# A decoder layer on one core: where the MLP's first weights, its raw rows and its normed rows lie, and from which unit on the normed rows are used

## The chip, the cores and the metric

The kernel runs on one core of a Trainium2 chip. TensorE (PE in the profile) multiplies matrices and writes its sums to PSUM banks; PEld is its weight load. VectorE (DVE), ScalarE (ACT) and GpSimd (POOL) work on tiles in SBUF and PSUM, and SyncE (SP) issues the DMAs. Each engine has an instruction list of its own, fixed when the program is built, and semaphores tie the lists together. The metric is the device time of one execution in microseconds; the median of three runs is compared.

## The reference

One layer of a decoder (256 positions of 1024 channels, all float32): a norm, one input projection, three kinds of attention, a gated merge, an output projection and a residual; then the part that matters here:

```python
x = x + merged.astype(x.dtype) @ w_out[i]
x = x + conv_ffn(rmsnorm(x, norm_ffn[i]), w_up[i], conv_w[i], conv_b[i], w_down[i])
return rmsnorm(x, norm_final)

def conv_ffn(x, w_up, conv_w, conv_b, w_down):
    h = x @ w_up                       # 1024 -> 2 * 2816
    h = causal depthwise conv of width 3 over h, + conv_b
    a, u = jnp.split(h, 2, axis=-1)
    return (jax.nn.silu(a) * u) @ w_down
```

## The kernel before

**Split numbers.** Every weight arrives by DMA as a raw float32 block of 1 MB (a "unit", 128 x 2048). ScalarE writes its rounded part `whi` (`Unit.hi`, L222, two halves of 128x1024), VectorE the rest, `wlo = raw - whi` (`Unit.lo`, L226, two halves). Activations are split in the same way. A product is then three matmuls: low by high, high by low, high by high (`mm3`, L237 to L240).

**The rings.** Raw blocks and split parts come from rings of buffers: `next_tile` (L156) walks through two pools, and once attention is closed five pairs of split parts are to be had. A unit's split waits until the pair that it takes over has been read for the last time. `turns[1]` counts the pairs given out.

**Big activation buffers.** Two buffers of 128 x 4096 float32 are reused by name. `hn` (pool `acts`) holds the mixer's normed rows, high and low, which every projection of the mixer reads, the gates' at the end too (L384 to L396, L443). `parts` (pool `mix`) holds attention's split output (L491), which the branch projections read (L801). In the MLP `hn` holds the raw turned rows (the residual stream, transposed and multiplied by the norm's weight, not yet by 1/rms; L830) and `parts` holds the normed rows (L868).

**The MLP.** It has 11 units of 256 hidden channels. Unit i uses three weight units: `fa{i}` and `fu{i}` (the two halves of `w_up`) and `fd{i}` (`w_down`). For each of its two channel blocks `up` (L980) runs once on `fa` and once on `fu`, `conv` (L963) does the width-3 convolution (one activation on ScalarE, L965, two operations on VectorE, L967), silu and product follow (L1001, L1003), the result is split into `fh` and `fl` (L1006, L1007), and `later` (L760) queues its 12 products with `fd`, written to the four `acc` banks.

**Two forms of `up`.** For i < NORMED the raw turned rows are the moving operand, 24 matmuls of 256 columns, and VectorE multiplies the result by 1/rms (`by_rstd`, L861, L864). From i = NORMED on the normed rows are used: high and low part lie side by side, so that `whi` takes both in one matmul of 512 columns (L988) and `wlo` the high part in one of 256 (L990), 16 matmuls in all; ScalarE copies one half of the bank out (L996) and VectorE adds the other (L997). The normed rows are made by `norm_parts` (L874), called at i = NORMED - 1: for each of two halves one multiplication (L876), one rounding on ScalarE (L877) and one subtraction (L878).

**What sets the order.** From the last products of the output projection to the first conv of the MLP the order is written by hand (`manual_schedule`, L891 to L951; unit 0's four `up`s are `first_products` there). Before and after it a scheduler at build time sorts the instructions of each engine by its own estimates, starting from the order in which they are written. SP's list is that of the DMA issues; its rows are the same in the kernel before and after.

Of the kernel before, what the change touches and what calls it, by code (L numbers as in the profile page):

```python
# [11 lines left out]
F32R = mybir.dt.float32r  # L12
# [3 lines left out]

P = 128
WARM = 9
NORMED = 3
S = 256  # L20
D = 1024
KC = D // P
# [107 lines left out]
def decoder_layer(ctx: ExitStack, tc, x, small_b, table, w1, wts, norms, out):  # L130
# [5 lines left out]
    act_pool = ctx.enter_context(tc.tile_pool(name="acts", bufs=1))  # L136
# [15 lines left out]
    UW = 2048  # L152
    wpools = [(wpool, 4, 2)]
    turns = [0, 0]

    def next_tile(dtype, name, which):  # L156

        names = [w for w in wpools for _ in range(w[which])]
        pool = names[turns[which - 1] % len(names)]
        return pool[0].tile([P, UW], dtype, name=name, bufs=pool[which])  # L160

    def raw_tile():
        t = next_tile(F32, "raw", 1)
        turns[0] += 1
        return t
# [39 lines left out]
    class Unit:  # L205


        def __init__(self, name, cuts=1):
            at, k, n = places[name]
            self.size = k * n  # L210
            self.raw = raw_tile()
            self.parts = next_tile(F32R, "whi", 2), next_tile(F32R, "wlo", 2)
            turns[1] += 1
            src = wts[at:at + P * k * n].rearrange("(p n) -> p n", p=P)
            for i in range(cuts):
                sl = slice(k * n * i // cuts, k * n * (i + 1) // cuts)
                nc.sync.dma_start(self.raw[:, sl], src[:, sl])
            self.views = [t[:, :k * n].rearrange("p (k n) -> p k n", k=k) for t in self.parts]
# [15 lines left out]
    def unit(name, steps=2, eng=None):  # L234
        return Unit(name).split(steps, eng)

    def mm3(ps, ah, al, bh, bl, start, stop):  # L237
        nc.tensor.matmul(ps, al, bh, start=start, stop=False)  # L238
        nc.tensor.matmul(ps, ah, bl, start=False, stop=False)  # L239
        nc.tensor.matmul(ps, ah, bh, start=False, stop=stop)  # L240

    mix = ctx.enter_context(tc.tile_pool(name="mix", bufs=1))
# [60 lines left out]
    with tc.manual_schedule(engines={mybir.EngineType.Activation, mybir.EngineType.DVE, mybir.EngineType.Pool,  # L303
# [77 lines left out]
        h_parts = act_pool.tile([P, KC, 2, S], F32R, name="hn")  # L381
# [338 lines left out]
    def gates(n, pool=psg):  # L720

        out = []
        for b in range(3):
            gl = mix.tile([P, 4, S], F32, name="gl", bufs=4).rearrange("p a b -> p (a b)").rearrange("p (t n) -> p t n", t=NT)
            pss = by_rows([f"g{n}{b}{i}" for i in range(2)], 512, pool)
            for t in range(NT):
                nc.scalar.activation(gl[:, t, :], pss[t], AF.Copy)
            out.append(gl)
        return out
# [12 lines left out]
    def bank():  # L742
        turn[0] ^= 1
        return pools[turn[0]].tile([P, 512], F32, name="g")
# [15 lines left out]
    def later(acc, ah, al, w, c, start, stop, depth):  # L760

        def emit(t, n, c0=0, c1=512, own=None):
            cols = slice(n * 512 + c0, n * 512 + c1)
            ps, first = (acc[t][n], start) if own is None else (own, waiting[0] is emit)
            mm3(ps[:, c0:c1], ah[:, t * P:(t + 1) * P], al[:, t * P:(t + 1) * P],
                w[0][:, c, cols], w[1][:, c, cols], first, stop)
        waiting.append(emit)
        while len(waiting) > depth:
            e = waiting.pop(0)
            for t in range(NT):  # L770
                for n in range(2):
                    e(t, n)
# [8 lines left out]
    for n in range(2):  # L781
        if n:
            gl.append(gates(n, psg2))
        br = [unit(f"br{n}{i}") for i in range(2)]
        uo = [unit(f"wo{2 * n + i}") for i in range(2)]
        if n:
            first = {"fa0": unit("fa0")}
            u_f = Unit("fu0")
            for j in range(2):
                u_f.hi(j, 2)  # L790
            first["fu0"] = u_f.views
        for b in range(3):
            nc.scalar.activation(gl[n][b], gl[n][b], AF.Sigmoid)
        mg = [gl[n][0][:, t, :] for t in range(NT)]
        for t in range(NT):
            rows = slice(t * P, (t + 1) * P)
            for b, (k0, k1) in enumerate(branch_k):
                ps = psg.tile([P, 512], F32, name="g")
                for k in range(k0, k1):
                    u = br[k // 4]  # L800
                    mm3(ps, o_hi[:, k, rows], o_lo[:, k, rows], u[0][:, k % 4, :], u[1][:, k % 4, :], k == k0, k == k1 - 1)  # L801
                nc.vector.tensor_mul(gl[n][b][:, t, :], ps, gl[n][b][:, t, :])
                if b:
                    nc.vector.tensor_add(mg[t], mg[t], gl[n][b][:, t, :])

        for i in range(2):
            ps = psg.tile([P, 512], F32, name="g")
            for c in range(2):
                for t in range(NT):
                    nc.tensor.transpose(ps[:, c * S + t * P:c * S + (t + 1) * P], mg[t][:, (2 * i + c) * P:(2 * i + c + 1) * P],  # L810
                                        ident)
            mh = mpool.tile([P, 2, S], F32R, name="mh", bufs=3)
            ml = mpool.tile([P, 2, S], F32R, name="ml", bufs=3)
            ps = ps.rearrange("p (c q) -> p c q", c=2)
            nc.scalar.activation(mh, ps, AF.Copy)
            nc.vector.tensor_sub(ml, ps, mh.bitcast(F32))
            for c in range(2):
                dc = 4 * n + 2 * i + c
                later(acc, mh[:, c, :], ml[:, c, :], uo[i], c, dc == 0, dc == KC - 1, 4)
# [7 lines left out]
            parts.append(square_mean(xs[:, t, sl], junk[:, sl], f"{tag}{t}{n}"))  # L827
        return rstd_of(parts, f"{tag}{t}")

    h_raw = act_pool.tile([P, KC, 2, S], F32R, name="hn")  # L830
    h_hi, h_lo = h_raw[:, :, 0, :], h_raw[:, :, 1, :]
    spare = [act_pool.tile([P, D], F32, name=f"xn{t}") for t in range(NT)]
    rows, scaled = spare[1][:, 0:S], [spare[1][:, i * S:(i + 1) * S] for i in range(1, 4)]
# [31 lines left out]
        return u  # L865


    h_parts = mix.tile([P, KC, 2, S], F32R, name="parts")  # L868
    whole = [mix.tile([P, 4, S], F32, name="gl", bufs=4) for _ in range(2)]

    def weighted_T(c):
# [91 lines left out]
    def conv(u, ch):  # L963
        y = mpool.tile([P, S], F32, name="cy", bufs=3)
        on_act.append(nc.scalar.activation(y, u, AF.Identity, bias=vec_c[:, 3, ch:ch + 1], scale=vec_c[:, 2, ch:ch + 1]))  # L965
        for w, sh in ((1, 1), (0, 2)):
            nc.vector.scalar_tensor_tensor(y[:, sh:], u[:, :S - sh], vec_c[:, w, ch:ch + 1], y[:, sh:],  # L967
                                           op0=ALU.mult, op1=ALU.add)
        return y

    for i in range(NFF // 2):
        with tc.issue_after(on_act[3 + i].ins) if i in (1, 2) else ExitStack():
            ua, uu, ud = [fu.pop(f"f{w}{i}", None) or unit(f"f{w}{i}") for w in "aud"]
        if i == NORMED - 1:
            for part in range(2):
                norm_parts(part)
        for c in range(2):
            ch = 2 * i + c

            def up(u):  # L980
                cols = slice(c * P, (c + 1) * P)
                ps = bank()
                if i < NORMED:
                    for k in range(KC):
                        mm3(ps[:, :S], u[0][:, k, cols], u[1][:, k, cols], h_hi[:, k, :], h_lo[:, k, :], k == 0, k == KC - 1)
                    return by_rstd(ps[:, :S])
                for k in range(KC):
                    hi = lambda: nc.tensor.matmul(ps, u[0][:, k, cols], h_parts[:, k].rearrange("p a q -> p (a q)"),  # L988
                                                  start=k == 0, stop=k == KC - 1)
                    lo = lambda: nc.tensor.matmul(ps[:, :S], u[1][:, k, cols], h_parts[:, k, 0, :], start=False, stop=False)  # L990
                    for product in ((lo, hi) if k else (hi, lo)):
                        product()
                v, part = scaled.pop(0), copies.pop(0)
                scaled.append(v)
                copies.append(part)
                nc.scalar.activation(part, ps[:, S:], AF.Copy)  # L996
                nc.vector.tensor_add(v, ps[:, :S], part)  # L997
                return v
            a = conv(firsts[2 * ch] if ch < 2 else up(ua), ch)
# [87 lines left out]
```

## Time and profile before

| | us |
|---|---|
| median of three runs (lowest, highest) | 424.69 (424.49, 424.78) |
| the profiled execution's own time | 424.76 |
| its span, first to last instruction | 423.0 |
| PE busy in the span | 412.4 (98%) |
| DVE busy | 313.2 (74%) |
| ACT busy | 256.2 (61%) |
| mean granted TensorE clock | 0.996 |

The span is what the rows of the trace add up to; about 1.8 us lie around it. A row of a timeline gives the start, the time until its last instruction ends, the engine, line, operation, tiles and shape, how many equal instructions it merges, and in brackets the idle time before it and who ended it. Consecutive instructions overlap a little: an engine starts the next one before the last has quite ended, so the distance from start to start is what one instruction costs in a queue.

### The profile page before, as it was taken

To read this page: it belongs to the slowest core of one execution; us is meant where nothing else is said; L and a number is where in the kernel's file an instruction comes from. 1 tells how busy PE (TensorE), PEld (TensorE's weight loads), DVE (VectorE), ACT (ScalarE), POOL (GpSimd) and SP (SyncE) were. 2 spreads that over 40 slices of the span, in tenths; PEclk is the share of its full clock that TensorE was granted. 3 is DMA by queue.
4 is the path that set the end of the run, shared out by engine and by line. 5 is a ranking of instruction groups with operands and counts; after the bars stand their busy time and mean duration, and the time that the engine had idled before them with its cause. 6 is when DMAs were issued, how large, how long until landed. Compare 5 with 4: busy or idle time off the path is not lost.

```text
span 423.0 us, 6337 instructions
## 1 busy us (share of the span) xinstructions
PE 412.4 (98%) x2407; PEld 347.8 (82%) x2407; DVE 313.2 (74%) x624; ACT 256.2 (61%) x451; POOL 18.3 (4%) x28
## 2 busy tenths in 40 slices
PE   8999999999999999999999999999999999999993
PEld 7998778776667888878788998988888888888883
DVE  3996653788784888434753899998797797887765
ACT  5843283547787855555434889467476576584633
POOL 2500010120000000000000000000000000000001
PEclk9999999999999999999999999999999999999998
DMA  8999419532227793645350465565652743800002
GB/s 279 416 375 407 146 34 354 198 131 100 101 100 248 292 381 109 229 184 198 107 192 0 149 253 198 200 251 200 245 212 105 283 187 110 299 0 2 0 2 99
DMA packets 12750, 78.00 MB, mean 184 GB/s; under 512 B 1408, under 2 KB 1424, under 8 KB 4912
## 3 DMA queue, kind: packets, MB, share of 16 engines
q1 hardware_dynamic: 12144, 75.48, 47.8%
q0 software_dynamic: 576, 2.12, 1.4%
q8 instruction: 19, 0.31, 0.3%
q14 instruction: 11, 0.09, 0.1%
HBM read 76.52 MB, written 1.07 MB: 183 GB/s over the span
## 4 chain that ended last, share of the span: by engine, by line
PE 82%; DVE 8%; ACT 5%; DMA 2%; issue 2%; SPq 0%; POOLq 0%; POOL 0%; ACTq 0%
PE g L988 12%; PE g L239 10%; PE g L240 10%; PE g L238 10%; PE g L990 6%; PE acc L238 6%; PE acc L240 6%; PE acc L239 6%; PE g L298 3%; DVE wlo L226 2%; PE g L888 2%; PE o L541 2%; DMA raw<-in_wts_dram 2%; PE g L426 2%; PE g L300 1%
## 5 line engine op out<-in xcount | busy, mean ns | idle before, releaser
L226 DVE TENSOR_TENSOR wlo<-raw,whi 128x1024 fp32r<-128x1024 f32 (+2 forms) x131 | 154.1, 1201 | 41.0 <-ACT whi L222 40.6
L222 ACT ACTIVATE whi<-raw 128x1024 fp32r<-128x1024 f32 (+2 forms) x130 | 130.2, 1040 | 50.5 <-PE g L240 34.3
L988 PE MATMUL g<-parts,whi 128*128 128x512 f32 x256 | 89.4, 396 | 0.0
L990 PE MATMUL g<-parts,wlo 128*128 128x256 f32 x256 | 66.2, 279 | 0.0
L988 PEld LDWEIGHTS g<-parts,whi 128*128 128x128 f32 x256 | 46.7, 188 | 9.2
L990 PEld LDWEIGHTS g<-parts,wlo 128*128 128x128 f32 x256 | 48.2, 188 | 2.8
L239 PE MATMUL g<-wlo,hn 128*128 128x512 f32 (+1 forms) x128 | 50.0, 391 | 0.0
L240 PE MATMUL g<-whi,hn 128*128 128x512 f32 (+1 forms) x128 | 50.0, 391 | 0.0
L238 PE MATMUL g<-whi,hn 128*128 128x512 f32 (+1 forms) x128 | 49.8, 390 | 0.0
L967 DVE SCALAR_TENSOR_TENSOR cy<-xn,small_b,cy 128x255 f32<-128x255 f32 (+1 forms) x88 | 41.5, 480 | 9.0 <-ACT cy L965 8.0
L238 PE MATMUL acc<-whi,fl 128*128 128x512 f32 (+1 forms) x88 | 34.2, 389 | 0.1
L239 PE MATMUL acc<-wlo,fh 128*128 128x512 f32 (+1 forms) x88 | 34.0, 386 | 0.0
L240 PE MATMUL acc<-whi,fh 128*128 128x512 f32 (+1 forms) x88 | 34.0, 386 | 0.0
L965 ACT ACTIVATE cy<-xn,small_b 128x256 f32<-128x256 f32 x44 | 25.8, 598 | 7.4 <-DVE xn L997 7.4
L239 PEld LDWEIGHTS g<-wlo,hn 128*128 128x128 f32 x128 | 24.1, 188 | 5.1 <-issue 0.9
L240 PEld LDWEIGHTS g<-whi,hn 128*128 128x128 f32 x128 | 24.1, 188 | 4.2 <-issue 0.2
L238 PEld LDWEIGHTS g<-whi,hn 128*128 128x128 f32 x128 | 24.1, 189 | 4.0 <-ACT whi L222 0.2
L426 PE MATMUL g<-hn,whi 128*128 128x512 f32 x72 | 26.2, 405 | 0.0
L996 ACT ACTIVATE xn<-g 128x256 f32<-128x256 f32 x32 | 12.2, 380 | 22.2 <-PE g L988 22.2
L428 PE MATMUL g<-hn,wlo 128*128 128x256 f32 x72 | 19.9, 292 | 0.0
L997 DVE TENSOR_TENSOR xn<-g,xn 128x256 f32<-128x256 f32 x32 | 13.5, 421 | 8.3 <-ACT xn L996 8.3
L240 PEld LDWEIGHTS acc<-whi,fh 128*128 128x128 f32 x88 | 16.5, 188 | 3.4
(213 smaller groups left out, 698.6 us busy)
## 6 DMA issues: line engine op xcount, KB each, us to landing
raw<-in_wts_dram SPq DMA_DIRECT2D x61, 1024.0 KB, 4.8
gl<-in_w_dram SPq DMA_DIRECT2D x8, 512.0 KB, 7.6
raw<-in_wts_dram SPq DMA_DIRECT2D x5, 512.0 KB, 7.4
raw<-in_wts_dram SPq DMA_DIRECT2D x2, 804.0 KB, 9.0
T<-tvd POOLq DMA_DIRECT2D x1, 1280.0 KB, 16.3
xs<-in_x_dram SPq DMA_DIRECT2D x2, 516.0 KB, 3.8
out_dram<-raw SPq DMA_DIRECT2D x4, 256.0 KB, 2.1
T<-tvd POOLq DMA_DIRECT2D x1, 768.0 KB, 9.6
```

What stands on the lines that cost most here:

```text
L222: nc.scalar.activation(self.parts[0][:, sl], self.raw[:, sl], AF.Copy)
L226: return (eng or nc.vector).tensor_sub(self.parts[1][:, sl], self.raw[:, sl], self.parts[0][:, sl].bitcast(F32))
L238: nc.tensor.matmul(ps, al, bh, start=start, stop=False)
L239: nc.tensor.matmul(ps, ah, bl, start=False, stop=False)
L240: nc.tensor.matmul(ps, ah, bh, start=False, stop=stop)
L426: hi = lambda: nc.tensor.matmul(ps, view(0, k), h_parts[:, k].rearrange("p a q -> p (a q)"), start=k == 0, stop=k == KC - 1)
L428: lo = lambda: nc.tensor.matmul(ps[:, :S], view(1, k), h_hi[:, k, :], start=False, stop=False)
L965: on_act.append(nc.scalar.activation(y, u, AF.Identity, bias=vec_c[:, 3, ch:ch + 1], scale=vec_c[:, 2, ch:ch + 1]))
L967: nc.vector.scalar_tensor_tensor(y[:, sh:], u[:, :S - sh], vec_c[:, w, ch:ch + 1], y[:, sh:], op0=ALU.mult, op1=ALU.add)
L988: hi = lambda: nc.tensor.matmul(ps, u[0][:, k, cols], h_parts[:, k].rearrange("p a q -> p (a q)"), start=k == 0, stop=k == KC - 1)
L990: lo = lambda: nc.tensor.matmul(ps[:, :S], u[1][:, k, cols], h_parts[:, k, 0, :], start=False, stop=False)
L997: nc.vector.tensor_add(v, ps[:, :S], part)
```

## The change

Three edits. `fa0`'s two split parts no longer take a pair of the ring but lie in the room of the mixer's normed rows (`hn`), which the last gate product reads; the ring's counter does not move for it, so every later unit takes the pair that the unit before it took. The raw turned rows go to `parts`, the normed rows to `hn`. NORMED goes from 3 to 2: the third unit (i = 2) runs on the normed rows, and `norm_parts` is called one unit earlier.

```diff
--- before.py
+++ after.py
@@ -16,7 +16,7 @@
 
 P = 128
 WARM = 9
-NORMED = 3
+NORMED = 2
 S = 256
 D = 1024
 KC = D // P
@@ -205,12 +205,12 @@
     class Unit:
 
 
-        def __init__(self, name, cuts=1):
+        def __init__(self, name, cuts=1, parts=None):
             at, k, n = places[name]
             self.size = k * n
             self.raw = raw_tile()
-            self.parts = next_tile(F32R, "whi", 2), next_tile(F32R, "wlo", 2)
-            turns[1] += 1
+            self.parts = parts or (next_tile(F32R, "whi", 2), next_tile(F32R, "wlo", 2))
+            turns[1] += not parts
             src = wts[at:at + P * k * n].rearrange("(p n) -> p n", p=P)
             for i in range(cuts):
                 sl = slice(k * n * i // cuts, k * n * (i + 1) // cuts)
@@ -784,7 +784,9 @@
         br = [unit(f"br{n}{i}") for i in range(2)]
         uo = [unit(f"wo{2 * n + i}") for i in range(2)]
         if n:
-            first = {"fa0": unit("fa0")}
+
+            room = act_pool.tile([P, KC, 2, S], F32R, name="hn").rearrange("p k a q -> p (k a q)")
+            first = {"fa0": Unit("fa0", parts=(room[:, :UW], room[:, UW:])).split(2, None)}
             u_f = Unit("fu0")
             for j in range(2):
                 u_f.hi(j, 2)
@@ -827,7 +829,7 @@
             parts.append(square_mean(xs[:, t, sl], junk[:, sl], f"{tag}{t}{n}"))
         return rstd_of(parts, f"{tag}{t}")
 
-    h_raw = act_pool.tile([P, KC, 2, S], F32R, name="hn")
+    h_raw = mix.tile([P, KC, 2, S], F32R, name="parts")
     h_hi, h_lo = h_raw[:, :, 0, :], h_raw[:, :, 1, :]
     spare = [act_pool.tile([P, D], F32, name=f"xn{t}") for t in range(NT)]
     rows, scaled = spare[1][:, 0:S], [spare[1][:, i * S:(i + 1) * S] for i in range(1, 4)]
@@ -865,7 +867,7 @@
         return u
 
 
-    h_parts = mix.tile([P, KC, 2, S], F32R, name="parts")
+    h_parts = act_pool.tile([P, KC, 2, S], F32R, name="hn")
     whole = [mix.tile([P, 4, S], F32, name="gl", bufs=4) for _ in range(2)]
 
     def weighted_T(c):
```

Line numbers behind L788 are larger by two in the changed kernel (L864 becomes L866, and so on).

On VectorE the first conv operations of unit 0 open this stretch; it ends, in the kernel before, with the first half of the subtraction that makes `wlo` of `fa2` (L226 in the last row; the two L226 rows above it are `fd1`'s):

```order
L967 SCALAR_TENSOR_TENSOR cy<-xn_2267,small_b,cy 128x255 x2
L967 SCALAR_TENSOR_TENSOR cy<-xn_2267,small_b,cy 128x254 x2
L967 SCALAR_TENSOR_TENSOR cy<-xn_2267,small_b,cy 128x255
L864 TENSOR_TENSOR xn_2267<-g,xn_2267 128x256
L967 SCALAR_TENSOR_TENSOR cy<-xn_2267,small_b,cy 128x254
L864 TENSOR_TENSOR xn_2267<-g,xn_2267 128x256
L1003 TENSOR_TENSOR sa<-sa,cy 128x256
L864 TENSOR_TENSOR xn_2267<-g,xn_2267 128x256
L876 TENSOR_TENSOR gl<-gl,xn_2267 128x1024
L1007 TENSOR_TENSOR fl<-sa,fh 128x256
L967 SCALAR_TENSOR_TENSOR cy<-xn_2267,small_b,cy 128x255
```

```order
L226 TENSOR_TENSOR wlo<-raw,whi 128x1024
L967 SCALAR_TENSOR_TENSOR cy<-xn_2267,small_b,cy 128x254
L226 TENSOR_TENSOR wlo<-raw,whi 128x1024
L1003 TENSOR_TENSOR sa<-sa,cy 128x256
L967 SCALAR_TENSOR_TENSOR cy<-xn_2267,small_b,cy 128x255 x2
L1007 TENSOR_TENSOR fl<-sa,fh 128x256
L967 SCALAR_TENSOR_TENSOR cy<-xn_2267,small_b,cy 128x254 x2
L864 TENSOR_TENSOR xn_2267<-g,xn_2267 128x256
L226 TENSOR_TENSOR wlo<-raw,whi 128x1024
```

In the changed kernel the same stretch stands so, in two pieces; the last row is again the first half of `wlo` of `fa2`:

```order
L969 SCALAR_TENSOR_TENSOR cy<-xn_2266,small_b,cy 128x255 x2
L969 SCALAR_TENSOR_TENSOR cy<-xn_2266,small_b,cy 128x254 x2
L969 SCALAR_TENSOR_TENSOR cy<-xn_2266,small_b,cy 128x255
L866 TENSOR_TENSOR xn_2266<-g,xn_2266 128x256
L969 SCALAR_TENSOR_TENSOR cy<-xn_2266,small_b,cy 128x254
L878 TENSOR_TENSOR gl<-gl,xn_2266 128x1024
L1005 TENSOR_TENSOR sa<-sa,cy 128x256
L969 SCALAR_TENSOR_TENSOR cy<-xn_2266,small_b,cy 128x255
L878 TENSOR_TENSOR gl<-gl,xn_2266 128x1024
L1009 TENSOR_TENSOR fl<-sa,fh 128x256
L969 SCALAR_TENSOR_TENSOR cy<-xn_2266,small_b,cy 128x254
L226 TENSOR_TENSOR wlo<-raw,whi 128x1024
```

```order
L1005 TENSOR_TENSOR sa<-sa,cy 128x256
L226 TENSOR_TENSOR wlo<-raw,whi 128x1024
L1009 TENSOR_TENSOR fl<-sa,fh 128x256
L880 TENSOR_TENSOR hn<-gl,hn 128x4x256 x2
L866 TENSOR_TENSOR xn_2266<-g,xn_2266 128x256 x3
L969 SCALAR_TENSOR_TENSOR cy<-xn_2266,small_b,cy 128x255 x2
L969 SCALAR_TENSOR_TENSOR cy<-xn_2266,small_b,cy 128x254 x2
L969 SCALAR_TENSOR_TENSOR cy<-xn_2266,small_b,cy 128x255
L866 TENSOR_TENSOR xn_2266<-g,xn_2266 128x256
L1005 TENSOR_TENSOR sa<-sa,cy 128x256
L969 SCALAR_TENSOR_TENSOR cy<-xn_2266,small_b,cy 128x254
L226 TENSOR_TENSOR wlo<-raw,whi 128x1024
```

Both multiplications of `norm_parts` (L878) and both subtractions (L880) now stand ahead of `wlo` of `fa2`, where one multiplication (L876) stood; two more conv operations (L969), one more by_rstd (L866) and one more silu product (L1005) stand ahead of it too.

On TensorE the third unit's first products stand between the last of unit 1's `up`s and the products of unit 1 with `fd1` (`acc`). Before, where the last four `g` rows are of `fa2`:

```order
L238 MATMUL g<-hn,wlo 128x256
L239 MATMUL g<-hn,whi 128x256
L240 MATMUL g<-hn,whi 128x256
L238 MATMUL g<-hn,wlo 128x256
L239 MATMUL g<-hn,whi 128x256
L240 MATMUL g<-hn,whi 128x256
L238 MATMUL g<-hn,wlo 128x256
L238 MATMUL acc_2523<-whi,fl 128x512
L239 MATMUL acc_2523<-wlo,fh 128x512
L240 MATMUL acc_2523<-whi,fh 128x512
```

And now, where the first three rows on `hn` are of `fa2`:

```order
L238 MATMUL g<-parts,wlo 128x256
L239 MATMUL g<-parts,whi 128x256
L240 MATMUL g<-parts,whi 128x256
L990 MATMUL g<-hn,whi 128x512 x2
L992 MATMUL g<-hn,wlo 128x256 x2
L990 MATMUL g<-hn,whi 128x512
L238 MATMUL acc_2522<-whi,fl 128x512
L239 MATMUL acc_2522<-wlo,fh 128x512
L240 MATMUL acc_2522<-whi,fh 128x512
```

Five products of `fa2` stand there instead of four; the first two, of 512 columns, need only `whi`, the third needs the first half of `wlo`.

## Rows read from the trace of the kernel before

**Rows 1.** Busy time of each engine by stretch: 240 to 280, the end

```profile
core 0: us, PE busy (x) PEld busy (x) DVE busy (x) ACT busy (x) POOL busy (x), PEclk, DMA share, GB/s
240.00:260.00 20.00, 20.00 (x147) 18.98 (x146) 19.43 (x35) 17.97 (x30) 0.00 (x0) 1.00 0.64 250
260.00:280.00 20.00, 20.00 (x138) 18.60 (x137) 19.84 (x32) 14.27 (x21) 0.00 (x0) 1.00 0.58 211
...
416.00:418.00 2.00, 0.53 (x5) 0.32 (x3) 1.50 (x5) 1.55 (x6) 0.15 (x1) 1.00 0.35 131
418.00:420.00 2.00, 0.00 (x0) 0.00 (x0) 0.75 (x1) 0.72 (x1) 0.40 (x1) 0.86 0.35 131
```

**Rows 2.** Timeline of PE where the third unit begins

```profile
260.34 0.28 PE L238 MATMUL g<-hn,wlo 128*128 128x256 f32 x1
...
260.82 0.40 PE L238 MATMUL acc<-whi,fl 128*128 128x512 f32 x1
```

**Rows 3.** Timeline of DVE from the first conv to the wlo of fa2

```profile
246.18 2.06 DVE L967 SCALAR_TENSOR_TENSOR cy<-xn,small_b,cy 128x255 f32<-128x255 f32 x5
248.15 0.42 DVE L864 TENSOR_TENSOR xn<-g,xn 128x256 f32<-128x256 f32 x1
...
249.95 1.22 DVE L876 TENSOR_TENSOR gl<-gl,xn 128x1024 f32<-128x1024 f32 x1
251.08 0.42 DVE L1007 TENSOR_TENSOR fl<-sa,fh 128x256 fp32r<-128x256 f32 x1
251.41 0.48 DVE L967 SCALAR_TENSOR_TENSOR cy<-xn,small_b,cy 128x255 f32<-128x255 f32 x1
...
257.06 1.21 DVE L226 TENSOR_TENSOR wlo<-raw,whi 128x1024 fp32r<-128x1024 f32 x1
```

**Rows 4.** Timeline of DVE where norm_parts ran before

```profile
267.31 1.22 DVE L878 TENSOR_TENSOR parts<-gl,parts 128x1024 fp32r<-128x1024 f32 x1
268.44 1.22 DVE L876 TENSOR_TENSOR gl<-gl,xn 128x1024 f32<-128x1024 f32 x1
```

**Rows 5.** Timeline of PE: two ups of unit 2, two of unit 4

```profile
271.59 0.28 PE L238 MATMUL g<-hn,wlo 128*128 128x256 f32 x1
...
277.34 0.40 PE L988 MATMUL g<-parts,whi 128*128 128x512 f32 x1
...
296.78 0.39 PE L988 MATMUL g<-parts,whi 128*128 128x512 f32 x1
...
302.37 0.39 PE L238 MATMUL acc<-whi,fl 128*128 128x512 f32 x1
```

**Rows 6.** Timeline of ACT: splits of wo3, fa0, wo2, fu0; three convs

```profile
198.43 2.00 ACT L222 ACTIVATE whi<-raw 128x1024 fp32r<-128x1024 f32 x2
...
206.94 2.01 ACT L222 ACTIVATE whi<-raw 128x1024 fp32r<-128x1024 f32 x2 [5.57 <-PE g L240]
209.66 2.01 ACT L222 ACTIVATE whi<-raw 128x1024 fp32r<-128x1024 f32 x2 [0.71 <-PE g L240]
...
218.85 2.01 ACT L222 ACTIVATE whi<-raw 128x1024 fp32r<-128x1024 f32 x2 [1.78 <-PE acc L240]
...
243.90 1.61 ACT L965 ACTIVATE cy<-xn,small_b 128x256 f32<-128x256 f32 x3
```

**Rows 7.** Timeline of PE: the last product on the mixer's normed rows

```profile
197.51 0.39 PE L240 MATMUL g<-whi,hn 128*128 128x512 f32 x1
```

**Rows 8.** Timeline of SP: the issue of fa2's raw block

```profile
213.29 0.33 SPq L217 DMA_DIRECT2D raw<-in_wts_dram  x1
```

**Rows 9.** Timeline of DVE in the hand-written stretch: idle before the row

```profile
221.57 0.69 DVE L838 TENSOR_TENSOR xs<-acc,xs 128x512 f32<-128x512 f32 x1 [3.67 <-PE acc L240]
...
227.03 0.69 DVE L838 TENSOR_TENSOR xs<-acc,xs 128x512 f32<-128x512 f32 x1 [2.04 <-PE acc L240]
...
240.64 0.42 DVE L864 TENSOR_TENSOR xn<-g,xn 128x256 f32<-128x256 f32 x1 [0.57 <-PE g L946]
```

## The prediction

> **What bounds the kernel now.** First the busy times by stretch [rows 1]: between 240 and 280 PE is busy for 20.00 of every 20 us, and DVE for 19.43 and 19.84. PE sets the time, but in this stretch DVE has no time to spare either: 0.73 us idle in 40. Next the two timelines at the place where the third unit begins. PE starts its first product on `fa2` at 260.34 and goes on at 260.82 with unit 1's products [rows 2]. The first half of `wlo` of `fa2`, which that product reads, is the DVE row at 257.06 that lasts 1.21 us [rows 3]: ready at 258.27, so DVE is 260.34 - 258.27 = 2.07 us ahead of PE there. That lead is all the change has to spend. Last come the ACT rows of the splits in front of the MLP [rows 6]: ACT idles 5.57 us before `fa0`'s and 1.78 us before `fu0`'s, waiting for a pair of the ring, but PE is busy throughout, so these waits cost nothing now.
>
> **The room for fa0.** The edit removes the 5.57 us wait: the last product on the mixer's normed rows starts at 197.51 and takes 0.39 us [rows 7], so `hn` is free at 197.9. `fa0` can be rounded as soon as ACT is done with `wo3` (198.43 + 2.00, about 200.4), 6.5 us earlier than the 206.94 of before, and `fu0`, which now takes the pair that `fa0` took, at about 207 to 209 instead of 218.85 [rows 6]. Nobody takes up the gain: `fa0` is first read behind the output projection, and the low halves of `fu0` stay where the hand-written order has them. I count 0 us. In return `wo2`'s rounding is 2 us later, since the scheduler puts ten of the output projection's products ahead of the last branch products, and DVE subtracts `fa0` ahead of the merge. `wo2`, rounded from about 211.7 instead of 209.66, still comes well before the output projection's last products, which alone read it. At the turns of the merge PE may wait for DVE: between nothing and 0.3 us; I take 0.1, nearest to the order as it stands, where PE still has products between the turns.
>
> **The two activation rooms.** `parts` is free after the last branch product and `hn` after `fa0`'s last product, both long before the new owners write. 0 us, hidden by PE's output projection and by unit 0. SP's list has the same rows; `fa2`'s transfer is issued at 213.29 [rows 8], 47 us before it is needed, and may be a few us later at no cost.
>
> **Side by side in unit 2.** Four `up`s go from 24 matmuls of 256 columns to 8 of 512 and 8 of 256, the same 6144 columns. Two `up`s of unit 2 take 277.34 - 271.59 = 5.75 us; two `up`s in the other form take 302.37 - 296.78 = 5.59 us [rows 5]. The saving is 2 x 0.16 = 0.32 us on PE. The trace's own spacing agrees: 5.75 / 48 = 0.120 us for 256 columns, which is 13 ns above 256 / 2.4 GHz. The Trainium skill, page "TensorE: Matmul & The Clock Gate", section "Back-to-back issue gap", gives N / 2.4 + 2.5 ns instead; by it the 32 matmuls saved would be worth 0.08 us, an estimate from that page, and the sum below would come out 0.24 us higher. The rows show five times that overhead, so I keep 0.32.
>
> **norm_parts one unit earlier.** This is the term that decides. DVE works through its list in order, and the order rows of the change show what now stands ahead of `wlo` of `fa2`, counted from the first conv of unit 0. Cost per operation, start to start [rows 3]: a conv operation 1.97 / 5 = 0.394 (five rows between 246.18 and 248.15), a 128x256 operation 0.33 (251.08 to 251.41; I use 0.335), a 128x1024 one 1.13 (249.95 to 251.08); a subtraction of `norm_parts` has the same 1.13 [rows 4]. Before: 12 conv, 8 short (four by_rstd, two silu products, two `fl`), 3 long (one multiplication, two `wlo` halves of `fd1`): 4.73 + 2.68 + 3.39 = 10.80, and 246.18 + 10.80 = 256.98, where the trace has 257.06, so the count explains the stretch within 0.08. After: 14 conv, 10 short, 6 long: 5.52 + 3.35 + 6.78 = 15.65. `wlo` starts at 261.83 plus the 0.08 that was not explained and about 0.1 for new waits on ACT, and ends 1.21 later: near 263.2. The start at 246.18 itself does not move, since everything ahead of it is in the hand-written order.
>
> PE, unhindered, would reach 260.34 as before, do the two 512-column products that need only `whi` (2 x 0.227 = 0.45) and want `wlo` at 260.8. It waits 263.2 - 260.8 = 2.4 us. ACT is late too, but less: `whi` of `fa2` stands behind three convs, which wait for the by_rstd behind the two subtractions. By the same costs the first of these by_rstd runs at 246.18 + 11.6 = 257.8; ACT's three convs from 258.3 take 1.6 [rows 6], and half a rounding (2.00 / 2) ends near 260.9, 0.6 us after PE wants it. This lies inside the 2.4 and is not added. Behind the waiting product on PE stand unit 1's twelve `acc` products and the rest of the kernel; PE is full to the end, so nothing gives the 2.4 us back.
>
> **The sum.** + 2.4 (pause) + 0.1 (turns) - 0.32 (side by side) = + 2.2 us. The profiled execution took 424.76, 0.07 above the median, span 423.0; I expect a span of 425.2 and a median of 424.69 + 2.2 = **426.9**.
>
> **Bounds.** The pause is a difference of two sums of fifteen us; 2% of one is 0.3. If DVE or ACT meets waits of its own among the new neighbours, add up to 0.5; if L880, which writes `hn`, were shorter than its twin, take off up to 0.3. So 426.3 to 427.5 if the mechanism holds.
>
> **Rivals.**
> - *No pause, same time.* The place is DVE's list before 246.18. DVE idles there for PE several times, 3.67 us at 221.57, 2.04 at 227.03, 0.57 at 240.64 [rows 9]. If the earlier splits of `fa0` and `fu0` moved enough of DVE's work into these holes, it would reach the first conv early and the lead would be kept. It decides from 2.4 us earlier on; the price is then 424.69 + 0.1 - 0.32 = 424.5. Against it: the four subtractions between the holes and the conv are bound in the hand-written order behind operations that wait for PE. I give it 7%.
> - *A second pause.* DVE is busy 19.84 of 20 us in the next stretch [rows 1], so it comes out of the pause with little lead, and `wlo` of `fu2` or the `fl` of unit 1 could hold PE again. For it: a lead of 2.07 us was eaten once. Against it: from 264 to 272 DVE no longer has `norm_parts` to do, one multiplication and two subtractions, 3 x 1.13 = 3.4 us [rows 4], so it regains ground just there. It would add up to 1.2: 428.1. 5%.
> - *The clock falls in the pause.* At the end PE stops near 416.5; the granted clock is still 1.00 in 416 to 418 and 0.86 on average in 418 to 420 [rows 1], the lower level being 1.2 GHz. The pause that I expect has a part of 1.8 us without any product, shorter than the idle time that the end shows at full clock. Should it fall all the same, each us at the lower level loses half a us, and no row shows how long it would stay; with 2 to 4 us at that level 1 to 2 us more: 427.9 to 428.9. 3%.
>
> **How the numbers follow.** Forecast 85%, no pause 7%, second pause 5%, clock 3%. A measurement of this kernel tells 0.2% from no change, 0.85 us, so same is 423.84 to 425.54. The forecast and the last two rivals are slower; the first rival, at 424.5, is the same, unless it also gains at the turns of the merge. Slower 0.91 (85 and 8, less 2 for a pause of a third of the size), same 0.07, faster 0.02. The range takes the forecast's own 426.3 to 427.5, half a pause below and half a second pause above: 425.6 to 427.8.
>
> **What would show it.** In the profile after: a hole on PE of about 2.4 us in two parts (0.6 behind unit 1's last `up`, on `whi`; 1.8 before the first L992, on `wlo`), near 260 to 263.3; the DVE row of `wlo` for `fa2` starting near 262, behind two L880 rows near 255.5 and 256.6; unit 2's `up`s in 2.79 us each instead of 2.88; no PE hole between 197 and 231 above 0.3; the granted clock at 1.00 through 260 to 270. If PE shows no hole at the third unit's start, the lead was larger than I read it, and the step on `norm_parts` is wrong. If the hole is there and the time is not longer, PE had slack that rows 1 do not show.

## The result: slower by 0.6%, and what the profile after shows

| | before | after |
|---|---|---|
| median of six runs, side by side (us) | 424.9 (424.49 to 426.62) | 428.29 (426.91 to 428.75) |
| ratio to before, 95% interval | | 1.0065 (1.0046 to 1.0084) |
| the profiled execution, its span (us) | 424.76, 423.0 | 428.09, 426.3 |
| mean granted TensorE clock | 0.996 | 0.993 |

The forecast was 426.9, slower; it is slower, but the median lies above the range of 425.6 to 427.8. The times of the changed kernel come in two groups: over its 18 executions in three comparisons nine lie between 426.80 and 427.39 us (mean clock 0.996 to 0.998) and nine between 428.09 and 428.86 (0.992 to 0.994), so a median of six says mostly which group had more. The medians of the second and third comparison are 427.25 and 427.92; whether such a median lies inside the forecast's range or above it is luck. The ratios of those two comparisons are 1.006 (1.0042 to 1.0078) and 1.0067 (1.0046 to 1.0088). In the table the two medians alone stand 0.8% apart, more than the ratio says, because four of the six executions after lie in the later group and one of the six before lies near 426.6.

First the timeline of PE where the third unit begins, which answers [rows 2] (start, time, engine, line, operation, tiles, count; in brackets the idle time before it and who ended it):

```profile
259.73 0.28 PE L240 MATMUL g<-parts,whi 128*128 128x256 f32 x1
260.37 0.73 PE L990 MATMUL g<-hn,whi 128*128 128x512 f32 x2 [0.36 <-ACT whi L222]
262.82 0.50 PE L992 MATMUL g<-hn,wlo 128*128 128x256 f32 x2 [1.72 <-DVE wlo L226]
263.17 0.41 PE L990 MATMUL g<-hn,whi 128*128 128x512 f32 x1
263.39 0.61 PE L238 MATMUL acc<-whi,fl 128*128 128x512 f32 x1
263.80 0.63 PE L239 MATMUL acc<-wlo,fh 128*128 128x512 f32 x1
...
266.36 0.60 PE L239 MATMUL acc<-wlo,fh 128*128 128x512 f32 x1
266.79 0.41 PE L240 MATMUL acc<-whi,fh 128*128 128x512 f32 x1
267.04 0.40 PE L238 MATMUL acc<-whi,fl 128*128 128x512 f32 x1
```

There is the hole, in two parts. The last `up` product of unit 1 has its place to 259.85 (259.73 + 0.12), so 0.52 us go on `whi`; the two products take to 260.82, so 2.00 go on `wlo`. The pair of L992 then takes 0.35 to the next start instead of 2 x 0.12, which is another 0.11; its cause was not traced. Behind the hole comes what the forecast had at 3%: eight `acc` products stand 0.43 us apart instead of 0.23. The windows of the same execution say why (us, PE and PEld and DVE and ACT and POOL busy, granted clock, DMA share, GB/s); the first two answer to [rows 1]:

```profile
240.00:260.00 20.00, 20.00 (x144) 18.73 (x143) 19.84 (x33) 14.19 (x25) 0.00 (x0) 1.00 0.62 240
260.00:280.00 20.00, 17.92 (x85) 14.83 (x85) 18.36 (x30) 14.80 (x24) 0.00 (x0) 0.91 0.57 211
...
262.00:263.00 1.00, 0.17 (x1) 0.18 (x2) 1.00 (x2) 1.00 (x3) 0.00 (x0) 1.00 0.00 0
263.00:264.00 1.00, 1.00 (x5) 0.87 (x6) 1.00 (x3) 1.00 (x2) 0.00 (x0) 0.70 0.00 0
264.00:266.00 2.00, 2.00 (x7) 1.52 (x6) 2.00 (x3) 2.00 (x3) 0.00 (x0) 0.50 0.17 33
266.00:267.00 1.00, 1.00 (x4) 0.80 (x3) 1.00 (x3) 1.00 (x2) 0.00 (x0) 0.60 0.90 246
```

The clock is at its lower level of 1.2 GHz from about 263.4 to 266.8 (a window of 1 us at 0.70 has 0.6 us of it at 0.5). From 259.85 to 262.82 PE had done two products, 0.45 us of work; the clock fell 0.6 us after PE had started again. PE is shown as fully busy in the low stretch: busy time alone hides it.

DVE's timeline answers to [rows 3]: the first conv, the two subtractions of `norm_parts`, five conv operations, and the first half of `wlo` of `fa2`.

```profile
245.63 2.06 DVE L969 SCALAR_TENSOR_TENSOR cy<-xn,small_b,cy 128x255 f32<-128x255 f32 x5
...
255.00 2.35 DVE L880 TENSOR_TENSOR hn<-gl,hn 128x1024 fp32r<-128x1024 f32 x2
...
258.42 2.16 DVE L969 SCALAR_TENSOR_TENSOR cy<-xn,small_b,cy 128x255 f32<-128x255 f32 x5
...
261.55 1.22 DVE L226 TENSOR_TENSOR wlo<-raw,whi 128x1024 fp32r<-128x1024 f32 x1
```

From the first conv to `wlo` it is now 261.55 - 245.63 = 15.92 us (10.88 before; the forecast counted 15.83). On ACT, the splits in front of the MLP [rows 6] moved as forecast, `fa0`, `fu0` and `wo2` in this order, and no row of PE between 196 and 259 has a wait:

```profile
199.74 2.00 ACT L222 ACTIVATE hn<-raw 128x1024 fp32r<-128x1024 f32 x2
...
208.64 2.01 ACT L222 ACTIVATE whi<-raw 128x1024 fp32r<-128x1024 f32 x2 [5.96 <-PE g L240]
211.37 2.01 ACT L222 ACTIVATE whi<-raw 128x1024 fp32r<-128x1024 f32 x2 [0.72 <-PE g L240]
```

### The profile page after: what moved, and what is told of

Read it like the earlier page. It is cut to its first block, busy times and chain, and to the rows that moved or that the text cites. A ratio compares the mean times of both kernels' runs of the same rounds, so it can differ in the third digit from the quotient of the medians.

```text
span 426.3 us, 6277 instructions
## 1 busy us (share of the span) xinstructions
PE 413.3 (97%) x2375; PEld 345.8 (81%) x2375; DVE 314.1 (74%) x624; ACT 257.1 (60%) x455; POOL 19.7 (5%) x28
## 4 chain that ended last, share of the span: by engine, by line
PE 77%; DVE 12%; ACT 5%; issue 2%; DMA 2%; SPq 0%; POOLq 0%; POOL 0%; ACTq 0%; DVEq 0%
PE g L990 13%; PE g L239 8%; PE g L240 8%; PE g L238 8%; PE g L992 7%; PE acc L238 6%; PE acc L239 5%; PE acc L240 5%; DVE wlo L226 4%; PE g L298 3%; DVE cy L969 2%; PE g L890 2%; PE o L541 2%; PE g L426 2%; DMA raw<-in_wts_dram 2%
## 5 line engine op out<-in xcount | busy, mean ns | idle before, releaser
L226 DVE TENSOR_TENSOR wlo<-raw,whi 128x1024 fp32r<-128x1024 f32 (+2 forms) x129 | 151.7, 1200 | 40.4 <-ACT whi L222 39.9
L222 ACT ACTIVATE whi<-raw 128x1024 fp32r<-128x1024 f32 (+2 forms) x128 | 128.3, 1040 | 50.4 <-PE g L240 34.1
L990 PE MATMUL g<-hn,whi 128*128 128x512 f32 x288 | 100.8, 396 | 0.4 <-ACT whi L222 0.4
L992 PE MATMUL g<-hn,wlo 128*128 128x256 f32 x288 | 74.5, 279 | 1.7 <-DVE wlo L226 1.7
L990 PEld LDWEIGHTS g<-hn,whi 128*128 128x128 f32 x288 | 52.5, 188 | 10.9 <-ACT whi L222 0.6
L992 PEld LDWEIGHTS g<-hn,wlo 128*128 128x128 f32 x288 | 54.2, 188 | 5.2 <-DVE wlo L226 2.2
L969 DVE SCALAR_TENSOR_TENSOR cy<-xn,small_b,cy 128x255 f32<-128x255 f32 (+1 forms) x88 | 41.7, 480 | 9.7 <-ACT cy L967 8.7
L998 ACT ACTIVATE xn<-g 128x256 f32<-128x256 f32 x36 | 13.7, 381 | 24.9 <-PE g L990 24.9
L426 PE MATMUL g<-hn,whi 128*128 128x512 f32 x72 | 26.2, 405 | 0.0
L999 DVE TENSOR_TENSOR xn<-g,xn 128x256 f32<-128x256 f32 x36 | 15.2, 421 | 10.6 <-ACT xn L998 10.6
L428 PE MATMUL g<-hn,wlo 128*128 128x256 f32 x72 | 19.9, 292 | 0.0
```

Source lines behind the costliest of these rows:

```text
L222: nc.scalar.activation(self.parts[0][:, sl], self.raw[:, sl], AF.Copy)
L226: return (eng or nc.vector).tensor_sub(self.parts[1][:, sl], self.raw[:, sl], self.parts[0][:, sl].bitcast(F32))
L426: hi = lambda: nc.tensor.matmul(ps, view(0, k), h_parts[:, k].rearrange("p a q -> p (a q)"), start=k == 0, stop=k == KC - 1)
L428: lo = lambda: nc.tensor.matmul(ps[:, :S], view(1, k), h_hi[:, k, :], start=False, stop=False)
```

## The experiments

The theory is that of the prediction: `norm_parts` uses up VectorE's lead, and PE pauses. The rivals are that the rooms cost the time, that the side-by-side form does, and, for the part beyond the forecast, that the clock has a cause of its own. Executions start a few tenths apart, so I compare one stretch of PE in each: from the start of the output projection's last product to the end of PE's last one. In the kernel before it is 230.21 to 416.53 (416.25 + 0.28), 186.32 us; in the changed kernel's first profile it is 229.66 to 419.87, 190.21 us. Its two ends, before and then after:

```profile
230.21 0.39 PE L240 MATMUL acc<-whi,mh 128*128 128x512 f32 x1
...
416.25 0.28 PE L240 MATMUL g<-whi,fh 128*128 128x256 f32 x1
```

```profile
229.66 0.39 PE L240 MATMUL acc<-whi,mh 128*128 128x512 f32 x1
...
419.59 0.28 PE L240 MATMUL g<-whi,fh 128*128 128x256 f32 x1
```

**Rooms alone.** The changed kernel with the third unit on raw rows again.

```diff
-NORMED = 2
+NORMED = 3
```

> The changed kernel with NORMED back at 3: only the two edits on the rooms stay. Theory (norm_parts one unit earlier stands ahead of the third unit's low half on VectorE): no wait of TensorE above 0.4 us at the third unit's start, granted clock 1.00 from 260 to 270, time within 0.2 us of the kernel before plus 0.1 for the merge's turns, so 424.6 to 425.2. Rival A (the rooms cost the time): 428 or more, with new holes on TensorE between 197 and 231.

Median 425.06 beside 425.01, ratio 1.0007 (0.9994 to 1.002); stretch 186.29, no wait of PE from 196 on, clock 1.00 to PE's end. Rival A falls: the first two edits cost and save nothing that the stretch shows (0.03 us). The 0.1 us that I set for the turns of the merge is not to be seen.

**The third unit alone.** The kernel before with only NORMED = 2.

> The kernel before with NORMED = 2 alone: old rooms, the third unit on normed rows. Theory: the same hole as in the changed kernel, 2.3 to 2.7 us in two parts (0.4 on whi, 1.7 on wlo) at the third unit's start; with the granted clock lower for some 3 us behind it, 427.8 to 428.6; without that fall, 426.4 to 427.0. Rival A (the rooms cost the time): 424.4, no hole.

Median 428.51 (426.75 to 428.83), ratio 1.0065 (1.0044 to 1.0087), stretch 188.61. PE's rows show the same hole:

```profile
262.28 0.73 PE L988 MATMUL g<-parts,whi 128*128 128x512 f32 x2 [0.39 <-ACT whi L222]
264.74 0.51 PE L990 MATMUL g<-parts,wlo 128*128 128x256 f32 x2 [1.73 <-DVE wlo L226]
```

One line makes the whole pause; the rooms are not needed for it. Its times come in the same two groups: two executions at 426.75 and 426.99, four at 428.43 to 428.83. But this execution, 428.43 us long, kept its clock behind the hole (1.00 from 264 to 268). Its fall was elsewhere, at PE's beginning:

```profile
11.00:12.00 1.00, 1.00 (x8) 1.00 (x8) 1.00 (x4) 1.00 (x3) 1.00 (x2) 0.68 1.05 438
12.00:14.00 2.00, 2.00 (x11) 2.00 (x11) 2.00 (x7) 2.00 (x4) 1.63 (x2) 0.50 1.00 417
14.00:15.00 1.00, 1.00 (x7) 1.00 (x7) 1.00 (x3) 0.99 (x3) 0.32 (x1) 0.62 1.09 439
```

**Work off VectorE, onto GpSimd.** The low half of `fd1` is made by GpSimd.

```diff
-ua, uu, ud = [fu.pop(f"f{w}{i}", None) or unit(f"f{w}{i}") for w in "aud"]
+ua, uu, ud = [fu.pop(f"f{w}{i}", None) or unit(f"f{w}{i}", eng=nc.gpsimd if (w, i) == ("d", 1) else None) for w in "aud"]
```

> The changed kernel, with the low half of fd1 (two subtractions of 128x1024) made by GpSimd instead of VectorE, so that 2 x 1.13 us leave VectorE's list ahead of the third unit's low half. Theory: the wait on that low half falls from 1.72 us to 0 to 0.4, the granted clock stays at 1.00 from 260 to 270, and the time is 424.2 to 425.0 (the side-by-side saving of 0.3 may then be seen). Rival B (the side-by-side form or the place of the normed rows costs TensorE time by itself, not the wait): still 427 or more.

A miss: 429.92, ratio 1.0107 (1.0074 to 1.0139). The wait on `wlo` is gone, but PE now waits 3.52 us for `fl`. GpSimd, DVE and PE:

```profile
251.34 5.97 POOL L226 TENSOR_TENSOR wlo<-raw,whi 128x1024 fp32r<-128x1024 f32 x2 [17.72 <-issue]
```

```profile
252.44 2.63 DVE L969 SCALAR_TENSOR_TENSOR cy<-xn,small_b,cy 128x254 f32<-128x254 f32 x1
254.99 0.41 DVE L866 TENSOR_TENSOR xn<-g,xn 128x256 f32<-128x256 f32 x1
255.33 2.27 DVE L1005 TENSOR_TENSOR sa<-sa,cy 128x256 f32<-128x256 f32 x1
```

```profile
256.46 0.28 PE L238 MATMUL g<-parts,wlo 128*128 128x256 f32 x1
260.25 0.80 PE L238 MATMUL acc<-whi,fl 128*128 128x512 f32 x1 [3.52 <-DVE fl L1009]
```

A conv operation of 0.48 us takes 2.63 and a product of 0.42 takes 2.27 while GpSimd works: VectorE loses 4.0 us to be rid of 2.27. The row between them, which reads one operand from PSUM (`g`), is not slowed. The Trainium skill, page "SBUF — State Buffer", section "Who interferes with whom", says that a VectorE instruction with two inputs in SBUF contends with a GpSimd instruction that reads SBUF, and it calls the port pair that the two engines share an exclusive lock. The three rows agree: the second slowed row ends at 257.60, 0.3 us after GpSimd's second subtraction (251.34 + 5.97 = 257.31). The run neither supports nor contradicts the theory, for it did not take VectorE's time away.

The run shows one more thing. The clock fell inside this wait, near 258.7 (0.93 on average from 257 to 259, 0.50 from 259 to 265), 2.0 us after the last product in front of it had ended (256.46 + 0.28):

```profile
257.00:259.00 2.00, 0.00 (x0) 0.00 (x0) 2.00 (x3) 1.37 (x3) 0.31 (x1) 0.93 0.34 53
```

**Work off VectorE, onto ScalarE.** In `norm_parts`:

```diff
-nc.vector.tensor_sub(h_parts[:, sl, 1, :], whole[i], h_parts[:, sl, 0, :].bitcast(F32))
+nc.scalar.activation(h_parts[:, sl, 1, :], whole[i], AF.Copy, scale=2.0 ** -12)
```

> The changed kernel with the two subtractions of norm_parts (2 x 1.13 us on VectorE) replaced by two scaled copies on ScalarE (2 x 0.95 us); the low part of the normed rows is therefore left out, and something small stands in its place. Theory (each us that leaves VectorE's list ahead of the third unit's low half leaves the pause): the wait on that low half falls from 1.72 us to nothing or 0.3, the one on ScalarE's half may grow from 0.36 to 1.0 by the copies; time 424.2 to 425.4. Rival B (the pause is not VectorE's list): 427 or more.

Median 425.10 beside 424.96, ratio 1.0009 (0.9995 to 1.0023); stretch 186.25. The hole is gone:

```profile
261.92 0.28 PE L240 MATMUL g<-parts,whi 128*128 128x256 f32 x1
262.04 0.63 PE L990 MATMUL g<-hn,whi 128*128 128x512 f32 x2
262.63 0.51 PE L992 MATMUL g<-hn,wlo 128*128 128x256 f32 x2
```

The low part of the normed rows is left out here. Without 2 x 1.13 us on VectorE, 2.63 us of hole (the two parts above and 0.11 in the first L992 pair) shrink to 262.63 - 262.04 - 0.45 = 0.14 and about the same 0.1 in that pair. Rival B falls: the third unit ran side by side here, at the old time.

**The pause filled.** Ten products more on PE in front of the third unit's first (their sum is thrown away).

```diff
+if i == NORMED and c == 0 and u is ua:
+    for _ in range(FILL):
+        nc.tensor.matmul(ps, h_hi[:, 0, 0:P], h_raw[:, 0].rearrange("p a q -> p (a q)"), start=True, stop=True)
```

> The changed kernel with ten extra products of 512 columns on TensorE in front of the third unit's first one; their sum goes into a bank that is started anew right after, so nothing else changes. Ten at 0.227 us are 2.3 us, about the length of the hole, and the lists of VectorE and ScalarE stay as they are. Theory on the clock (it fell because of the pause): wait on wlo 0.5 us or less, granted clock 1.00 from 260 to 270, the rest of the kernel as late as the pause alone makes it: 426.4 to 427.1. Rival C (the clock falls for another reason, or the extra time is not the clock's): 428.0 to 428.6, the clock below 1.00 in 263 to 267 as in the changed kernel.

```profile
262.05 2.46 PE L988 MATMUL g<-parts 128*128 128x512 f32 x10
264.35 0.61 PE L994 MATMUL g<-hn,whi 128*128 128x512 f32 x2
265.05 0.51 PE L996 MATMUL g<-hn,wlo 128*128 128x256 f32 x2
```

Median 427.69, four of six runs at 427.40 to 427.85, 0.3 us or more above the 426.4 to 427.1 expected; that excess was not traced. Stretch 188.61, the clock 1.00 from 260 to 270; the profiled execution (428.72) had a fall from 11 to 15 us. Inconclusive on the clock: an execution with an unfilled pause can keep its clock too (below). It shows that the lost time is the lateness of `wlo`, since the stretch is the same with or without work in the hole (188.61 here, 188.60 unfilled at full clock below).

**The changed kernel again, twice, for its clock.**

> The changed kernel once more, for its clock. Theory E (the clock falls behind the pause in most executions, 1.7 us each time): granted clock below 1.00 for some 3.4 us behind the pause near 263 to 267 again, and most runs at 428.1 to 428.8. Theory F (the pause alone makes 426.9; a fall elsewhere, as the one at 11 to 15 us in the run with NORMED alone, makes the rest): clock 1.00 behind the pause, and where the time is above 428 a stretch of lower clock in another place.

> The changed kernel a third time, for its clock behind the pause. Theory F (the pause alone makes 427.1; a fall of the clock comes on top in some executions, at 11 to 15 us or behind the pause, and costs 1.4 to 1.7 us): runs near 427.1 and near 428.6, none between but by 0.3. Theory E (a fall behind the pause in most executions): the clock below 1.00 behind the pause in this profile too, and five of six runs at 428 or more.

Medians 427.25 (427.09 to 428.85) and 427.92 (426.80 to 428.86). The first profile had the hole at full clock, with the fall at the beginning (0.50 from 12 to 14):

```profile
262.63 0.73 PE L990 MATMUL g<-hn,whi 128*128 128x512 f32 x2 [0.38 <-ACT whi L222]
265.09 0.50 PE L992 MATMUL g<-hn,wlo 128*128 128x256 f32 x2 [1.73 <-DVE wlo L226]
265.43 0.40 PE L990 MATMUL g<-hn,whi 128*128 128x512 f32 x1
265.67 0.39 PE L238 MATMUL acc<-whi,fl 128*128 128x512 f32 x1
```

Its stretch is 188.60. In the second the clock was 1.00 from 11 to 15 and fell at the end of the hole, near 263.2, where PE started again at 263.40; stretch 190.11:

```profile
11.00:15.00 4.00, 4.00 (x34) 4.00 (x35) 4.00 (x11) 4.00 (x8) 2.97 (x4) 1.00 1.02 421
263.00:264.00 1.00, 0.60 (x3) 0.60 (x4) 1.00 (x4) 1.00 (x2) 0.00 (x0) 0.58 0.00 0
264.00:266.00 2.00, 2.00 (x6) 1.61 (x6) 2.00 (x4) 2.00 (x4) 0.00 (x0) 0.50 0.00 0
```

So theory F: the pause is in all four profiles that have it unfilled and by itself makes the group near 427.1; a fall of the clock at the pause adds 1.5 to 1.6 (190.11 and 190.21 less 188.60), and an execution with a fall, at the pause or at the beginning, lies in the other group. Theory E falls, as four of six and three of six runs were near 427.1. The kernel before has the two groups too, only fewer of the later one: of the 23 executions timed beside this kernel's second comparison, 16 lie at 424.65 to 425.23 and 7 at 426.05 to 426.70 (clock 0.991 to 0.992). Between the earlier groups the difference is 427.1 - 424.9 = 2.2. A rough estimate of how often the clock falls at this pause: in the two kernels with it, 13 of 24 executions lie above 428, and in the kernel before, over its five comparisons, 19 of 86 lie above 426. The difference, about a third, is the share that the pause would add; the times do not show where an execution's fall was, so this is no measurement.

**The lead given back.** With the edits on the rooms `fu0` is rounded 10 us earlier (208.64 instead of 218.85), and DVE and ACT idle 4.77 and 7.23 us ahead of the first add-back (the addition of the output projection's result to the residual stream, L840). Whether the same could be had without these edits was not tried. In the hand-written order the low half of `fu0` and the split of `fa1` go there, and `fu1` takes `fa1`'s place, its low half ahead of the by_rstd operations instead of among them.

```diff
         sq = {}
+        for i in range(2):
+            u_f.lo(i, 2)
+        u_n = Unit("fa1")
+        fu["fa1"] = u_n.views
+        for i in range(2):
+            u_n.hi(i, 2)
+        for i in range(2):
+            u_n.lo(i, 2)
...
-        for i in range(2):
-            u_f.lo(i, 2)
-        u_n = Unit("fa1")
-        fu["fa1"] = u_n.views
+        u_n = Unit("fu1")
+        fu["fu1"] = u_n.views
```

> The changed kernel with its freed room used: in the hand-written order the low half of fu0 and both halves of fa1 stand ahead of the first add-back, where VectorE idles 4.77 us and ScalarE 7.23 us in the changed kernel, and the split of fu1 stands where fa1's stood. That takes four subtractions of 1.13 us out of VectorE's list between 234 and 246 us. Theory (the pause is VectorE's list, and its lead is all that decides): the first conv on VectorE comes 2 us or more earlier against TensorE, no wait above 0.3 us at the third unit's start, granted clock 1.00 from 255 to 270, and 424.1 to 424.8, that is 0.3 us below the kernel before at best. Rival B (the third unit on normed rows costs TensorE time however early VectorE is): 427 or more. Rival D (the new splits among the merge's work hold TensorE up in 204 to 216 instead): 425.0 to 426.5, with new holes there.

> The earlier splits with NORMED = 2 once more, on the same chip as the one with NORMED = 3. Theory: 424.1 to 424.5, the lowest of the three kernels, 0.3 to 0.6 us below the kernel before; the stretch from the output projection's last product to TensorE's end again 185.9 us. If 424.7 or more, the gain of the first time was chance.

> The earlier splits with NORMED = 2 a third time, beside the changed kernel on the same chip. Theory: 424.1 to 424.5 again, 0.4 to 0.7 us below the kernel before and 2.7 to 2.9 us below the changed kernel where neither has a fall of the clock; no wait at the third unit's start. If 424.7 or more, the gain is not established.

Medians 424.28, 424.32 and 424.23 beside 424.96, 424.80 and 424.92; ratios 0.9979 (0.9965 to 0.9993), 0.9993 (0.9975 to 1.001; one execution at 428.14) and 0.9981 (0.9968 to 0.9995). Each of these medians is 2.9 us or more below every median of the changed kernel. Below the kernel before, the times lie by about 0.2% in two comparisons of three; in the third the interval includes no difference. Part of that is the later group, to which fewer of its executions belong: counting only executions below 425.5, the medians stand 0.5 to 0.7 us apart in all three. DVE and PE of the first:

```profile
219.67 2.36 DVE L226 TENSOR_TENSOR wlo<-raw,whi 128x1024 fp32r<-128x1024 f32 x2 [1.10 <-ACT whi L222]
...
243.18 2.06 DVE L969 SCALAR_TENSOR_TENSOR cy<-xn,small_b,cy 128x255 f32<-128x255 f32 x5
...
256.67 1.22 DVE L226 TENSOR_TENSOR wlo<-raw,whi 128x1024 fp32r<-128x1024 f32 x1
```

```profile
260.04 0.39 PE L990 MATMUL g<-hn,whi 128*128 128x512 f32 x1
260.27 0.39 PE L238 MATMUL acc<-whi,fl 128*128 128x512 f32 x1
...
263.04 0.40 PE L992 MATMUL g<-hn,wlo 128*128 128x256 f32 x2
...
268.40 0.39 PE L238 MATMUL acc<-whi,fl 128*128 128x512 f32 x1
```

The conv starts 2.45 us earlier than in the changed kernel (2.7 against PE, whose stretch begins at 229.93 here and 229.66 there), `wlo` of `fa2` is ready at 257.9 and PE has no wait from 196 on, so rivals B and D fall. The earlier conv is only half of it: from there to `wlo` the list is 256.67 - 243.18 = 13.49 us long instead of 15.92, for in the new order one multiplication of `norm_parts` stands ahead of the conv, and a few more operations stand behind `wlo`. On PE the `acc` products now stand ahead of those on `wlo`. The run does not part these three; each of the first two is some 2.4 us by itself, more than the 2.00 us that PE waited on `wlo`. The stretch is 185.91, 185.88 and 185.86.

**The same with the third unit on raw rows**, NORMED = 3:

> The kernel with the earlier splits, but NORMED back at 3, so that the third unit runs on raw rows again. It tells whether the gain of the earlier splits comes from the third unit's side-by-side form or from the splits themselves. Theory (VectorE's lead is worth nothing by itself; the form saves 0.3 to 0.4 us on TensorE once the lead covers norm_parts): as the kernel before, 424.7 to 425.1, and from the output projection's last product to TensorE's end 186.2 to 186.4 us, against 185.91 with NORMED = 2. Rival G (the earlier splits save the time by themselves): 424.0 to 424.4.

Median 425.91 (424.31 to 427.21), ratio 1.0016 (0.9999 to 1.0032), stretch 186.45. Rival G falls: earlier splits alone save nothing. The median is above what I expected: five of twelve executions lie at 424.31 to 425.03, four at 425.74 to 426.68 with the clock of the later group (0.991 to 0.992; the profiled one has its fall at 11 to 15 us), and three between 426.08 and 427.21 at a mean clock of 0.994 to 0.997 I can't explain.

## Why the prediction was right, and where not

- *The lead and the list*: right. Two sums of DVE's rows gave 15.83 us; 15.92 came. Taking two subtractions out of the list takes the hole away, and so do the earlier splits, which put `wlo` 4.88 us earlier. A second pause did not come: PE has no wait behind 263.
- *The pause*: 2.4 forecast, 0.6 of it in front of the first product and 1.8 on `wlo`; measured 0.52 + 2.00 + 0.11 = 2.63.
- *Side by side*: 0.32 forecast. Two `up`s of unit 2 take 268.40 - 263.04 + 0.23 (the product done at 260.04) = 5.59 us, where [rows 5] has 5.75: twice 0.16, as forecast. The whole stretch without a hole is 0.41 to 0.46 shorter; the 0.1 beyond was not traced.
- *The rooms and the turns*: 0.1 forecast, nothing measured.
- *The sum*: +2.2 forecast; 188.60 - 186.32 = 2.28 in the stretch, 2.2 between the earlier groups of times. So the sum holds for an execution without a fall of the clock, half of the 18; for the other half it is some 1.6 too small.
- *The clock*: the step that failed. "The pause that I expect has a part of 1.8 us without any product, shorter than the idle time that the end shows at full clock." I took the end of one execution for a bound, gave the fall 3%, and read its price rightly: eight products at 0.43 instead of 0.23 are 1.6 us. The end is no bound. In the execution of [rows 1] the clock fell 2.9 us after PE's end; with the rooms alone it was 5.0 us (416.61, and about 421.6 by the first row), with the earlier splits 2.3 (415.84, and 418.1 by the second):

```profile
421.00:422.00 1.00, 0.00 (x0) 0.00 (x0) 0.00 (x0) 0.00 (x0) 0.00 (x0) 0.81 0.52 195
```

```profile
418.00:419.00 1.00, 0.00 (x0) 0.00 (x0) 0.50 (x1) 0.47 (x1) 0.00 (x0) 0.56 0.70 262
```

With `fd1` on GpSimd it was 2.0 us, inside a wait. I had also compared only the longest part of the pause, while PE did 0.45 us of work in 2.97 us. What the forecast did not reckon with at all is a fall at the beginning, which no row of the one profile before showed and the times of both kernels have. How often the clock falls at this pause, and what decides it, stays open: of the four profiles of it unfilled, two of the changed kernel have the fall there; the third of the changed kernel and the one with NORMED alone kept the clock there and had the fall at the beginning.

## What to carry to other kernels

Before work is moved earlier on an engine that is not the bottleneck, subtract: its lead at the place where the bottleneck reads from it, less the cost of all that the order now puts ahead. If the lead doesn't cover it, look for idle time of that engine further up; here the same change with four subtractions moved earlier came out about 0.2% faster in two comparisons of three, where it had cost 0.6%. Price a pause of TensorE of this size at its length, and beside it at its length plus one fall of the clock (1.5 to 1.6 us here), and give the fall a chance well above zero.

## What was not expected of the hardware

- The clock fell 0.6 us behind a pause in which PE worked 0.45 us of 2.97, and then stayed at 1.2 GHz for some 3.4 us under full work. In another execution of the same program it stayed at 2.4 GHz through the same pause.
- Some executions have a fall of the same size from about 11 to 15 us although PE is busy throughout it; it follows a stretch in which PE waits (busy 1.79 of the 4 us from 7 to 11 in the changed kernel's second profile). That wait alone does not decide it: with the rooms alone PE was busy 1.97 of these 4 us, and the clock stayed at 1.00.
- Two subtractions of 128x1024 on GpSimd took 5.97 us, against 2 x 1.13 on VectorE, and held up VectorE operations on two SBUF tiles by about 2 us each.
